# A decoder trunk on one core: VectorE's conditioning sums pinned in its order of issue, and spaced at 4500 columns in group B

## The chip, the cores and the metric

One core of a Trainium2 chip runs one program. The metric is the device time of one execution in microseconds, the median of a few runs of the same program. The engines are TensorE (PE: matmuls, with its weight loads listed as PEld), VectorE (DVE), ScalarE (ACT), GpSimd (POOL) and SyncE (SP), each with its own queue of instructions that it takes in order. SP issues most DMAs; POOL issues some.

## The reference, cut to what matters

One layer over 512 tokens of width 2048, batch 1, all in float32. The part that the change is about is the conditioning vector's product with a large matrix:

```python
c_act = jax.nn.silu(c)                    # (1, 2048)
mod = c_act @ w_mod[l] + b_mod[l]         # (1, 6 * 2048)
sh1, sc1, g1, sh2, sc2, g2 = split(mod, 6)
h = rms_norm(x, norm_attn[l]) * (1.0 + sc1) + sh1
...                                       # h @ w_in: queries and keys of groups A and B
x = x + g1 * (concat(out_A, out_B) @ w_out[l])
h = rms_norm(x, norm_ffn[l]) * (1.0 + sc2) + sh2
x = x + g2 * conv_ffn(h, w_up[l], conv_w[l], conv_b[l], w_down[l])
out = rms_norm(x, norm_final)
```

Group A is windowed attention of 16 heads; group B is attention of 16 heads over 128 keys for each query, chosen by an indexer (scores, then a top-k). The output projection is `w_out`, and the feed-forward part has 5632 hidden columns.

## The kernel before

Matrices are split into a high and a low part of a faster float type, and each product is three matmuls (`mm3`, L154). The weights come in tiles of 128x512 through a ring of buffers; ScalarE writes the high part, VectorE the low part (`split`, L147). TensorE takes the program's main stream of such tiles, "slots" (`drive`, L351), of 12 matmuls each: eight units of four slots for the queries of group A (qa0 to qa7), eight for group B (qb0 to qb7), sixteen for the output projection (wo0 to wo15), then the feed-forward part. Between slots generators advance by a step each. Attention runs as one of them: `pair_gen` (L802) takes two heads at a time through load, scores, softmax (VectorE adds the bias and takes the minimum into nm, ScalarE takes exp and divides), four-way transposes on TensorE (tpa, tpb), a copy by ScalarE to SBUF (eta, etb) and the product with the values (o). `prep_gen` (L881) makes keys kb and values vb of the next pair of B heads from wuk and wuv.

The conditioning product is cut into 24 groups of 512 columns (g = 0 to 23), each a sum of 16 pieces of 128x512. Groups 0 to 7 (shift and scale of the first norm) are done ahead of group A and don't concern us. For the others `mod_gen` (L233) loads a piece (tile mraw, 256 KB), and VectorE adds it, times one column of `cact`, to the accumulator macc (`mod_acc`, L199: L202 for the first piece, L204 for the other 15). After the sixteenth, `mod_cols` has TensorE add up macc's partitions in eight tiny matmuls (mps), and VectorE adds the bias (L251). Three such generators run:

- groups 8 to 13 beside group B of the attention (L1259): loads issued by POOL into the ring "mrw" of five buffers, so that piece n is loaded when the sum of piece n - 5 has given its buffer back. Groups 8 to 11 are the gate that the output projection needs.
- groups 14 to 19 beside the output projection (L1295): loads issued by POOL into eight buffers.
- groups 20 to 23 beside the feed-forward part (L1323): loads issued by SP into the ring "mrw" again.

`pace` (L266) sets at which point of the traced program a generator's step stands: each time that TensorE's counted columns have grown by a given number (5200, 3500 and 20000). But this is the place in the traced program alone. The framework's scheduler then puts each engine's instructions into their final order, by priority (the traced order) among those that its own estimate of times holds ready; an instruction whose operands it takes to be there early, as a sum whose block has been loaded, can be put far ahead of what was traced before it, and one that it takes for late can stand behind. The final order of each queue is fixed in the built program. On the chip each engine waits at the head of its queue for the semaphores of that instruction.

Of the kernel before, what the change touches and what calls it, by code (L numbers as in the profile page):

```python
# [11 lines left out]
OP = mybir.AluOpType  # L12
# [21 lines left out]
def hybrid_trunk(ctx, tc, xT, cT, wm, bm, nrm, wik, wiq, wi1, sinks, kvn, wuk, wuv, rel, onehot,  # L34
                 wo, wup, cw, cb, wdn, out):
    nc = tc.nc
    act, dve, pe, pool, sp = nc.scalar, nc.vector, nc.tensor, nc.gpsimd, nc.sync
# [63 lines left out]
    c_sb, sink_sb, bm_sb, nrm_sb = [t for t, _ in first.values()]  # L101
# [7 lines left out]
    cact = const.tile([P, KT], F32, name="cact")  # L109
# [5 lines left out]
    mod = const.tile([P, 24, 4], F32, name="mod")  # L115
# [83 lines left out]
    def mod_acc(accs, t, kt):  # L199
        acc = accs[kt % len(accs)]  # L200
        if kt < len(accs):
            dve.tensor_scalar(acc, t, cact[:, kt:kt + 1], None, OP.mult)  # L202
        else:
            dve.scalar_tensor_tensor(acc, t, cact[:, kt:kt + 1], acc, OP.mult, OP.add)  # L204

    def mod_rows(ps, t, q, start, stop):

# [9 lines left out]
    def mod_accs(g, mp, bufs, n=1):  # L217
        return [mp.tile([P, 512], F32, tag=f"macc{i}", bufs=1 if i else bufs, name=f"macc{g}_{i}") for i in range(n)]
# [14 lines left out]
    def mod_gen(groups, load, depth, mp, get, per):  # L233

        pieces = [(g, kt) for g in groups for kt in range(KT)]
        tiles = [load(*x) for x in pieces[:depth - 1]]
        n = 0
        for i, (g, kt) in enumerate(pieces):
            if i + depth - 1 < len(pieces):
                tiles.append(load(*pieces[i + depth - 1]))  # L240
            if kt == 0:
                acc = mod_accs(g, mp, 1)
            mod_acc(acc, tiles.pop(0), kt)
            n += 1
            if n % per == 0:
                yield
            if kt == KT - 1:
                ps = get(f"mps{g}")
                mod_cols(ps, acc)
                yield  # L250
                dve.tensor_tensor(mod[:, g], ps[:, 0:4], bm_sb[:, g], OP.add)  # L251


    active, idle = [], []
# [11 lines left out]
    def pace(gen, every):  # L266
        paced.append([gen, every, pe.cols])
# [29 lines left out]
    class Raw:  # L297
# [3 lines left out]
        def load(self, part):  # L301
            if part not in self.t:
                self.t[part] = load_raw(self.src[:, 512 * part:512 * part + 512], f"{self.name}_{part}")
# [264 lines left out]
    p1 = p1c.__enter__()  # L568
# [687 lines left out]
    drive(slots, marks["qb0"] - 4, marks["qb0"], True)  # L1256
    while idle:
        step()
    pace(mod_gen(range(8, 14), ring_mod, 5, p1, sc_ps, 1), 5200)  # L1259
    drive(slots, marks["qb0"], marks["wo"], True)  # L1260
    env["mh"] = mh = big.tile([P, KT, T], F32R, tag="b2", name="mh")
    env["ml"] = ml = big.tile([P, KT, T], F32R, tag="b3", name="ml")
# [158 lines left out]
```

## Time and profile before

| | us |
|---|---|
| median of 3 runs | 2219.88 (2218.86 to 2222.04) |
| profiled execution, its own time | 2221.85 |
| its span, first to last instruction | 2220.1 |

| stage (us of the span) | what TensorE works on |
|---|---|
| 0 to 186 | keys, indexer's queries, groups 0 to 7 of the conditioning |
| 186 to 386 | group A, indexer's scores and the top-k |
| 386 to 578 | group B |
| 578 to 800 | output projection, last heads of B at its start |
| 800 to 2220 | norm, feed-forward part, final norm |

The profile is read by stage: which engine is busy throughout, where that engine has idle time, and which instruction ended each idle time. The granted clock is TensorE's share of 2.4 GHz.

### The profile page before, as it was taken

To read this page: it belongs to the slowest core of one execution; us is meant where nothing else is said; L and a number is where in the kernel's file an instruction comes from. 1 tells how busy PE (TensorE), PEld (TensorE's weight loads), DVE (VectorE), ACT (ScalarE), POOL (GpSimd) and SP (SyncE) were. 2 spreads that over 40 slices of the span, in tenths; PEclk is the share of its full clock that TensorE was granted. 3 is DMA by queue.
4 is the path that set the end of the run, shared out by engine and by line. 5 is a ranking of instruction groups with operands and counts; after the bars stand their busy time and mean duration, and the time that the engine had idled before them with its cause. 6 is when DMAs were issued, how large, how long until landed. Compare 5 with 4: busy or idle time off the path is not lost.

```text
span 2220.1 us, 30149 instructions
## 1 busy us (share of the span) xinstructions
PE 2149.7 (97%) x10376; PEld 1750.1 (79%) x10376; DVE 1568.2 (71%) x2829; ACT 976.2 (44%) x1850; POOL 242.4 (11%) x376
## 2 busy tenths in 40 slices
PE   8999998999879999999999999999999999999997
PEld 4777776777768878888888888888888888888887
DVE  3887999566769765686867776675757666675666
ACT  5334877666722264334333343334334343333342
POOL 0000000111233200000201010110201010010200
PEclk9999999999989999999999999999999999999999
DMA  9783422454599734454757565563727465563672
GB/s 396 258 296 102 110 72 61 145 176 150 189 351 340 261 97 142 137 191 144 161 168 168 154 154 139 129 147 114 162 96 165 119 139 141 131 149 111 116 257 76
DMA packets 168921, 367.09 MB, mean 165 GB/s; under 512 B 20159, under 2 KB 27343, under 8 KB 162624
## 3 DMA queue, kind: packets, MB, share of 16 engines
q1 hardware_dynamic: 130208, 270.81, 36.9%
q0 software_dynamic: 37696, 92.79, 20.0%
q8 instruction: 81, 1.33, 0.2%
q10 hardware_dynamic: 864, 1.57, 0.2%
q14 instruction: 72, 0.59, 0.1%
HBM read 312.93 MB, written 52.17 MB: 164 GB/s over the span
## 4 chain that ended last, share of the span: by engine, by line
PE 79%; issue 13%; DMA 4%; DVE 2%; POOL 1%; ACT 1%; SPq 0%; POOLq 0%; DVEq 0%; ACTq 0%
PE p L53 17%; PE qip L53 3%; DMA mraw<-in_wm_dram 3%; POOL mraw L144 1%; PE ckv L53 1%; PE mps L53 1%; PE mrow L53 1%; DMA wiq<-in_wiq_dram 1%; DVE macc L204 1%; PE d_2ps L53 1%; PE u0ps L53 1%; PE g0ps L53 1%; PE d_0ps L53 1%; PE d_1ps L53 1%; PE wo15ps L53 0%
## 5 line engine op out<-in xcount | busy, mean ns | idle before, releaser
L190 ACT CAST dh<-rq 128x512 fp32r<-128x512 f32 x240 | 149.4, 623 | 172.0 <-PE p L53 140.5
L204 DVE SCALAR_TENSOR_TENSOR macc<-mraw,cact,macc 128x512 f32<-128x512 f32 x240 | 178.2, 748 | 39.4 <-DMA mraw<-in_wm_dram 36.5
L191 DVE TENSOR_TENSOR dl<-rq,dh 128x512 fp32r<-128x512 f32 x240 | 161.3, 685 | 40.0 <-ACT dh L190 39.1
L53 PE MATMUL p<-dh,ah 128*128 128x512 f32 x480 | 186.7, 389 | 0.0
L53 PE MATMUL p<-dl,ah 128*128 128x512 f32 x480 | 186.7, 389 | 0.0
L53 PE MATMUL p<-dh,al 128*128 128x512 f32 x480 | 186.7, 389 | 0.0
L1118 POOL DMA_DIRECT2D cd<-co x72 | 61.4, 858 | 878.6 <-DVE co L1131 876.2
L53 PEld LDWEIGHTS p<-dh,al 128*128 128x128 f32 x480 | 90.2, 188 | 18.7
L53 PEld LDWEIGHTS p<-dh,ah 128*128 128x128 f32 x480 | 90.1, 188 | 18.7
L53 PEld LDWEIGHTS p<-dl,ah 128*128 128x128 f32 x480 | 90.0, 188 | 18.8
L144 POOL DMA_DIRECT2D mraw<-in_wm_dram x96 | 51.6, 538 | 430.7 <-DVE macc L202 199.2
L1134 DVE TENSOR_TENSOR v<-p,v 128x512 f32<-128x512 f32 x120 | 82.3, 686 | 6.3 <-PE p L53 5.5
L1118 POOL DMA_DIRECT2D cd<-v x72 | 61.3, 856 | 128.4 <-DVE v L1136 76.2
L190 ACT CAST ah<-cu 128x256 fp32r<-128x256 f32 (+2 forms) x60 | 41.5, 692 | 50.5 <-DVE cu L1033 27.3
L1292 POOL DMA_DIRECT2D mraw<-in_wm_dram x96 | 51.4, 536 | 104.4 <-DVE macc L204 59.8
L191 DVE TENSOR_TENSOR al<-cu,ah 128x256 fp32r<-128x256 f32 (+2 forms) x60 | 46.7, 779 | 22.8 <-ACT ah L190 20.1
L1131 DVE TENSOR_TENSOR co<-p,v 128x512 f32<-128x512 f32 x80 | 54.9, 686 | 7.2 <-PE p L53 7.2
L1053 DVE TENSOR_TENSOR rq<-rq,rq 128x512 f32<-128x512 f32 x80 | 52.4, 685 | 1.4 <-DMA rq<-in_wdn_dram 1.4
L516 DVE TENSOR_TENSOR qi<-qi,qip 128x512 f32<-128x512 f32 x56 | 38.3, 684 | 14.4 <-PE qip L53 13.6
L778 ACT ACTIVATE sb<-sb,nmb 128x512 f32<-128x512 f32 (+2 forms) x64 | 35.3, 554 | 24.9 <-DVE nmb L776 21.4
L191 DVE TENSOR_TENSOR dl_t<-tw,dh_t 128x512 fp32r<-128x512 f32 x40 | 27.7, 692 | 22.5 <-ACT dh_t L190 22.5
L415 DVE SCALAR_TENSOR_TENSOR macc<-mraw,cact,macc 128x512 f32<-128x512 f32 x54 | 40.3, 747 | 0.4
(4492 smaller groups left out, 6396.2 us busy)
## 6 DMA issues: line engine op xcount, KB each, us to landing
mraw<-in_wm_dram POOLq DMA_DIRECT2D x192, 256.0 KB, 5.4
rq<-in_wdn_dram SPq DMA_DIRECT2D x160, 256.0 KB
mraw<-in_wm_dram SPq DMA_DIRECT2D x32, 1024.0 KB
cd<-co POOLq DMA_DIRECT2D x80, 256.0 KB, 4.8
cd<-v POOLq DMA_DIRECT2D x80, 256.0 KB, 4.7
mraw<-in_wm_dram SPq DMA_DIRECT2D x64, 256.0 KB
wiq<-in_wiq_dram SPq DMA_DIRECT2D x32, 256.0 KB
wik<-in_wik_dram SPq DMA_DIRECT2D x8, 592.0 KB
```

What stands on the lines that cost most here:

```text
L53: return self.to.matmul(out, w, x, **kw)
L144: by.dma_start(t, src)
L190: act.copy(hi_t, full)
L191: dve.tensor_tensor(lo_t, full, hi_t.bitcast(F32), OP.subtract)
L204: dve.scalar_tensor_tensor(acc, t, cact[:, kt:kt + 1], acc, OP.mult, OP.add)
L415: dve.scalar_tensor_tensor(acc, fetched[j, q][:, kt % 4], cact[:, kt:kt + 1], acc, OP.mult, OP.add)
L516: dve.tensor_tensor(qi[i], qi[i], ps, OP.add)
L1053: dve.tensor_tensor(self.b[out], self.b[a], self.b[b], OP.add)
L1118: pool.dma_start(cd[tb][dq], t, accum_op=OP.add)
L1131: dve.tensor_tensor(t, ps, box["v" if i == 1 else "u", b], OP.subtract)
L1134: dve.tensor_tensor(box["v", b], ps, box["v", b], OP.add)
L1292: pool.dma_start(t, wm[g, kt // 4][:, kt % 4])
```

## The change

`mod_acc`'s two forms of sum and the bias add of L251 are wrapped in `tc.keep_in_program_order`, which adds an edge without a semaphore: the scheduler must keep the instruction behind the one that was traced last before it on the same engine. This holds for groups 8 to 23. Instructions traced later can still be put ahead of a pinned one; nothing else is tied. And the generator beside group B takes its steps at every 4500 columns, where it was 5200. No operation is added or taken away.

```diff
--- before.py
+++ after.py
@@ -199,9 +199,9 @@
     def mod_acc(accs, t, kt):
         acc = accs[kt % len(accs)]
         if kt < len(accs):
-            dve.tensor_scalar(acc, t, cact[:, kt:kt + 1], None, OP.mult)
+            tc.keep_in_program_order(dve.tensor_scalar(acc, t, cact[:, kt:kt + 1], None, OP.mult))
         else:
-            dve.scalar_tensor_tensor(acc, t, cact[:, kt:kt + 1], acc, OP.mult, OP.add)
+            tc.keep_in_program_order(dve.scalar_tensor_tensor(acc, t, cact[:, kt:kt + 1], acc, OP.mult, OP.add))
 
     def mod_rows(ps, t, q, start, stop):
 
@@ -248,7 +248,7 @@
                 ps = get(f"mps{g}")
                 mod_cols(ps, acc)
                 yield
-                dve.tensor_tensor(mod[:, g], ps[:, 0:4], bm_sb[:, g], OP.add)
+                tc.keep_in_program_order(dve.tensor_tensor(mod[:, g], ps[:, 0:4], bm_sb[:, g], OP.add))
 
 
     active, idle = [], []
@@ -1256,7 +1256,7 @@
     drive(slots, marks["qb0"] - 4, marks["qb0"], True)
     while idle:
         step()
-    pace(mod_gen(range(8, 14), ring_mod, 5, p1, sc_ps, 1), 5200)
+    pace(mod_gen(range(8, 14), ring_mod, 5, p1, sc_ps, 1), 4500)
     drive(slots, marks["qb0"], marks["wo"], True)
     env["mh"] = mh = big.tile([P, KT, T], F32R, tag="b2", name="mh")
     env["ml"] = ml = big.tile([P, KT, T], F32R, tag="b3", name="ml")
```

Three places show how the built order moves. A name's last number is that of a buffer; `mraw9_12` is piece 12 of group 9.

VectorE in group B, near the end of group 9's sums. Names: macc is the accumulator, kb2 and qb2 are the keys and queries of the third pair's heads, `_l` are low parts of weights. Before:

```order
L204 SCALAR_TENSOR_TENSOR macc9_0_4147<-mraw9_10_4298,cact_99,macc9_0_4147 128x512
L204 SCALAR_TENSOR_TENSOR macc9_0_4147<-mraw9_11_4329,cact_99,macc9_0_4147 128x512
L204 SCALAR_TENSOR_TENSOR macc9_0_4147<-mraw9_12_4344,cact_99,macc9_0_4147 128x512
L602 TENSOR_TENSOR kb2_4268<-kbp2_4261,kb2_4268 64x512
L603 TENSOR_TENSOR kb2_4268<-kbp2_4261,kb2_4268 64x512
L587 SCALAR_TENSOR_TENSOR qb2_4280<-qb2ps_4029,qb2_4280 64x512
```

and with the change:

```order
L587 SCALAR_TENSOR_TENSOR qb2_4292<-qb2ps_4035,qb2_4292 64x512
L151 TENSOR_TENSOR qb3r_3l_4300<-qb3r_3_4158,qb3r_3h_4299 128x512
L602 TENSOR_TENSOR kb2_4277<-kbp2_4270,kb2_4277 64x512
L603 TENSOR_TENSOR kb2_4277<-kbp2_4270,kb2_4277 64x512
L204 SCALAR_TENSOR_TENSOR macc9_0_4089<-mraw9_8_4188,cact_99,macc9_0_4089 128x512
L587 SCALAR_TENSOR_TENSOR qb2_4292<-qb2ps_4035,qb2_4292 64x512
L204 SCALAR_TENSOR_TENSOR macc9_0_4089<-mraw9_9_4191,cact_99,macc9_0_4089 128x512
L151 TENSOR_TENSOR wuv2l_4331<-wuvr2_4147,wuv2h_4330 128x512
L204 SCALAR_TENSOR_TENSOR macc9_0_4089<-mraw9_10_4241,cact_99,macc9_0_4089 128x512
L151 TENSOR_TENSOR qb4r_0l_4347<-qb4r_0_4244,qb4r_0h_4346 128x512
L204 SCALAR_TENSOR_TENSOR macc9_0_4089<-mraw9_11_4256,cact_99,macc9_0_4089 128x512
L204 SCALAR_TENSOR_TENSOR macc9_0_4089<-mraw9_12_4286,cact_99,macc9_0_4089 128x512
```

Before, three sums stood in a row ahead of the first step of kb2; piece 12 stood seven rows behind piece 7, whose buffer its load takes. Now another instruction stands between any two of these sums, and piece 12 stands behind the steps of kb2 and qb2, 14 rows behind piece 7 (row 699, just ahead of these). Of the 80 pieces of groups 9 to 13, 19 stood at most nine rows behind the piece whose buffer they take; with the change 1 does (seven rows), and all others stand 14 rows or more behind. Group 8, whose sums stood in group A (rows 203 to 334 of VectorE's queue), has moved to the start of group B (617 to 670).

VectorE in the output projection, at the end of group 14. Before:

```order
L151 TENSOR_TENSOR wo4r_1l_6340<-wo4r_1_6291,wo4r_1h_6339 128x512
L204 SCALAR_TENSOR_TENSOR macc14_0_6145<-mraw14_14_6235,cact_99,macc14_0_6145 128x512
L204 SCALAR_TENSOR_TENSOR macc20_0_7961<-mraw20_5_8017,cact_99,macc20_0_7961 128x512
L204 SCALAR_TENSOR_TENSOR macc14_0_6145<-mraw14_15_6250,cact_99,macc14_0_6145 128x512
L151 TENSOR_TENSOR wo4r_2l_6366<-wo4r_2_6316,wo4r_2h_6365 128x512
L251 TENSOR_TENSOR mod_105<-mps14_6358,bm_sb_83 128x4
```

and with the change:

```order
L151 TENSOR_TENSOR wo4r_0l_6319<-wo4r_0_6262,wo4r_0h_6318 128x512
L204 SCALAR_TENSOR_TENSOR macc14_0_6145<-mraw14_14_6235,cact_99,macc14_0_6145 128x512
L151 TENSOR_TENSOR wo4r_1l_6340<-wo4r_1_6291,wo4r_1h_6339 128x512
L204 SCALAR_TENSOR_TENSOR macc14_0_6145<-mraw14_15_6250,cact_99,macc14_0_6145 128x512
L151 TENSOR_TENSOR wo4r_2l_6366<-wo4r_2_6316,wo4r_2h_6365 128x512
L251 TENSOR_TENSOR mod_105<-mps14_6358,bm_sb_83 128x4
```

Piece 5 of group 20 stood ahead of the last piece of group 14, and all sixteen pieces of group 20 stood in rows 969 to 1048, among those of groups 14 to 16. Now group 20 stands in rows 1220 to 1349, behind groups 14 to 19.

SP's queue, at the same place. Before:

```order
L144 DMA wo5r_2_6418<-in_wo_dram 128x512
L144 DMA mraw20_5_8017<-in_wm_dram 128x512
L144 DMA wo5r_3_6442<-in_wo_dram 128x512
L144 DMA mraw20_6_8081<-in_wm_dram 128x512
L144 DMA mraw20_7_8139<-in_wm_dram 128x512
L144 DMA wo6r_0_6466<-in_wo_dram 128x512
L144 DMA mraw20_8_8202<-in_wm_dram 128x512
```

and with the change:

```order
L144 DMA wo5r_2_6418<-in_wo_dram 128x512
L144 DMA wo5r_3_6442<-in_wo_dram 128x512
L144 DMA wo6r_0_6466<-in_wo_dram 128x512
L144 DMA wo6r_1_6494<-in_wo_dram 128x512
L1319 DMA x2d0_1659<-x2_0_6112 128x2048
L144 DMA wo6r_2_6519<-in_wo_dram 128x512
```

The loads of pieces 5 to 15 of group 20 and of pieces 0 to 4 of group 21 (16 loads of 256 KB) stood between the loads of wo5 to wo9. They now stand among those of the feed-forward part; pieces 0 to 4 of group 20 are still loaded at the start of the projection.

## Rows read from the trace of the kernel before

**Rows 1.** The page's first part: busy time of the span, its share and the number of instructions.

```profile
PE 2149.7 (97%) x10376; PEld 1750.1 (79%) x10376; DVE 1568.2 (71%) x2829; ACT 976.2 (44%) x1850; POOL 242.4 (11%) x376
```

**Rows 2.** The view of busy times in stretches that follow the stages (end of group A, group B, start of the output projection, its rest). Columns: stretch and its length, then busy us and instructions of each engine, the granted TensorE clock, the share of the DMA engines, GB/s.

```profile
186.00:386.00 200.00, 189.93 (x1079) 151.43 (x1077) 183.04 (x486) 150.79 (x387) 11.26 (x21) 0.98 0.32 88
386.00:578.00 192.00, 172.87 (x1046) 139.52 (x1045) 122.96 (x277) 127.74 (x304) 34.35 (x64) 0.95 0.55 168
578.00:660.00 82.00, 69.10 (x355) 54.66 (x356) 58.44 (x105) 35.44 (x76) 19.80 (x37) 0.88 0.76 275
660.00:800.00 140.00, 139.72 (x653) 116.53 (x652) 109.84 (x176) 40.01 (x64) 37.54 (x70) 1.00 0.79 272
```

**Rows 3.** The view of waits, TensorE alone, of 386 to 600 us: who waited for whom, us in total, times, the longest.

```profile
PE tpb L57 <- ACT etb L799: 8.7, 6, 2.6
PE o L53 <- ACT etb L799: 4.3, 2, 2.5
PE wo0ps L53 <- ACT mh L190: 3.3, 1, 3.3
PE kbp L53 <- DVE wuk7l L151: 3.0, 1, 3.0
```

**Rows 4.** The same view of TensorE, 600 to 800 us.

```profile
PE mps L53 <- DVE macc L204: 12.2, 2, 10.8
```

**Rows 5.** Busy times in the stretches in which the clock row of the profile shows 0.50, which is 1.2 of 2.4 GHz, with the same columns as rows 2.

```profile
444.80:448.20 3.40, 3.40 (x20) 2.97 (x15) 3.27 (x6) 1.17 (x2) 0.54 (x1) 0.50 0.29 100
496.00:499.40 3.40, 3.40 (x20) 2.35 (x20) 1.45 (x3) 0.87 (x2) 0.00 (x0) 0.50 0.29 104
530.10:533.50 3.40, 3.40 (x14) 3.11 (x13) 3.13 (x5) 1.17 (x2) 1.00 (x2) 0.51 0.46 158
574.50:584.70 10.20, 6.83 (x23) 5.36 (x21) 8.00 (x13) 8.66 (x18) 0.83 (x2) 0.50 0.42 137
646.20:659.80 13.60, 5.58 (x17) 4.83 (x18) 3.91 (x7) 0.08 (x1) 1.89 (x4) 0.50 0.88 314
```

**Rows 6.** The view of waits, VectorE alone, 386 to 600 us.

```profile
DVE macc L204 <- DMA mraw<-in_wm_dram: 21.5, 14, 3.6
...
DVE mod L251 <- PE mps L53: 2.3, 2, 1.6
```

**Rows 7.** The timeline of all engines, 439.5 to 444.5 us, in order of time: start, length, engine, line, operation, and in brackets the idle time before it and what ended that.

```profile
439.75 0.75 DVE L204 SCALAR_TENSOR_TENSOR macc<-mraw,cact,macc 128x512 f32<-128x512 f32 x1 [2.48 <-DMA mraw<-in_wm_dram]
...
440.42 0.68 DVE L602 TENSOR_TENSOR kb<-kbp,kb 64x512 fp32r<-64x512 f32 x1
...
441.82 0.58 ACT L599 CAST kb<-kbp 64x512 fp32r<-64x512 f32 x1 [2.44 <-DVE kb L603]
...
443.52 0.58 ACT L799 COPY etb<-tpb 128x512 f32<-128x512 f32 x1
...
444.15 0.55 PE L53 MATMUL o<-etb,vb 128*64 128x128 f32 x6 [1.87 <-ACT etb L799]
```

**Rows 8.** The timeline of all engines, 421 to 430 us: the first sum of group 9, the load that its buffer is next used for, and the sum that waits for that load.

```profile
421.74 0.48 DVE L202 TENSOR_SCALAR macc<-mraw,cact 128x512 f32<-128x512 f32 x1
...
422.52 0.56 POOL L144 DMA_DIRECT2D mraw<-in_wm_dram  x1 [127.39 <-DVE macc L202]
...
428.96 0.75 DVE L204 SCALAR_TENSOR_TENSOR macc<-mraw,cact,macc 128x512 f32<-128x512 f32 x1 [3.58 <-DMA mraw<-in_wm_dram]
```

**Rows 9.** The timeline of all engines, 637 to 657 us.

```profile
637.52 0.54 POOL L1292 DMA_DIRECT2D mraw<-in_wm_dram  x1 [0.18 <-issue]
...
640.82 0.43 SPq L144 DMA_DIRECT2D mraw<-in_wm_dram  x1
...
644.91 0.74 DVE L204 SCALAR_TENSOR_TENSOR macc<-mraw,cact,macc 128x512 f32<-128x512 f32 x1
...
652.66 1.42 DVE L204 SCALAR_TENSOR_TENSOR macc<-mraw,cact,macc 128x512 f32<-128x512 f32 x2 [7.01 <-DMA mraw<-in_wm_dram]
...
654.23 1.84 PE L53 MATMUL mps<-ones,macc 128*128 128x1 f32 x8 [10.77 <-DVE macc L204]
```

**Rows 10.** Busy times of 423 to 446 and 446 to 465 us, first of all instructions, then of those alone that read or write the accumulators macc (columns without POOL).

```profile
423.00:446.00 23.00, 18.57 (x115) 14.60 (x115) 16.17 (x33) 14.19 (x32) 6.51 (x13) 0.97 0.67 211
446.00:465.00 19.00, 19.00 (x122) 16.42 (x121) 8.94 (x27) 14.01 (x36) 1.61 (x3) 0.94 0.44 127
...
423.00:446.00 23.00, 0.00 (x0) 0.00 (x0) 8.26 (x12) 0.00 (x0) 0.97 0.67 211
446.00:465.00 19.00, 0.95 (x8) 1.05 (x8) 2.74 (x4) 0.00 (x0) 0.94 0.44 127
```

**Rows 11.** The DMA view of 600 to 660 us: GB/s in 40 slices of 1.5 us, and the last line of the view of tile mraw in 613 to 660 us and in 420 to 600 us (the time to landing of the loads that POOL issues).

```profile
GB/s 361 249 171 206 228 212 296 244 262 340 314 183 302 367 397 341 408 451 441 415 401 432 431 412 416 408 407 412 410 415 411 414 407 407 411 303 79 143 384 259
...
DMA to landing us min/median/max: 3.9/7.0/9.0
...
DMA to landing us min/median/max: 3.3/5.9/8.7
```

**Rows 12.** The view of tile mraw over the whole span: the sum on VectorE and the issue of the loads on POOL (shortest, median, longest in ns; first and last start).

```profile
L204 DVE SCALAR_TENSOR_TENSOR macc<-mraw,cact,macc x240: 722/749/755, 191.9 to 1283.0; 128x512 f32<-128x512 f32 x120
...
L144 POOL DMA_DIRECT2D mraw<-in_wm_dram x96: 536/536/613, 157.0 to 612.4; - x96
```

**Rows 13.** The view of waits, TensorE alone, of 186 to 386 us.

```profile
PE tpa L57 <- ACT sa L791: 5.3, 3, 2.9
```


## The prediction

> **What bounds the kernel now.** I read four views in this order: the page's busy times, the stretches by stage, the waits of TensorE by stage, and then the timeline at the longest waits. The first says that TensorE is busy 97% of the span [rows 1], so no edit of VectorE's queue can bring more than TensorE's idle time and its half-speed time. The stretches say where that is: TensorE was idle for 10 us of the 200 of group A, 19 us of the 192 of group B, 13 us of the 82 at the projection's start, and for next to nothing after 660 us [rows 2]. What TensorE waits for in each of these:
>
> - Group B and the start of the projection: transposes and products that need a copy by ScalarE (tpb 8.7, o 4.3), the first projection slot's wait for mh (3.3), keys that need the low part of wuk7 (3.0), 19.3 us together [rows 3].
> - Projection: the column sums mps wait for an accumulator, 1.4 us once and 10.8 us once [rows 4].
> - Group A's end: the transposes tpa, 5.3 us [rows 13], where VectorE is busy for 183 of 200 us [rows 2].
>
> Behind several of these the granted clock fell to 0.50, that is 1.2 GHz. Over those stretches TensorE was busy 3.40 (three times), 6.83 and 5.58 us [rows 5]; half of it is lost, 11.3 us in all: 5.1 in group B, 3.4 around the first projection slots, 2.8 behind the long mps wait.
>
> Who makes ScalarE late in group B? VectorE, mostly: its sums waited 21.5 us, in 14 waits, for their blocks [rows 6]. One instance is whole in the timeline: a sum waits 2.48 us for its DMA at 439.75, the step of kb behind it in VectorE's queue ends late, ScalarE's cast of kb has waited 2.44 us for it, the copy etb comes behind that in ScalarE's queue, and TensorE starts o 1.87 us late [rows 7]. The sum waits because five buffers are used faster than they come back: a buffer was free at 422.22, POOL issued its load at 422.52, and the sum that needed it began at 428.96, after 3.58 us of wait [rows 8]. Release to use is thus 6.7 us there. The sums come in clumps: 12 of them in 423 to 446 us, where TensorE is busy 18.6 of 23 us, and 4 in 446 to 465 us, where it is busy throughout [rows 10].
>
> **The change, part by part.**
>
> *1. Group B's waits.* With sums pinned at 4500 columns, one comes every 4500 / 2400 per us = 1.88 us of TensorE at full clock, and five buffers give a load 9.4 us from release to use. The row shows 6.7 us needed [rows 8], and POOL's loads here land in 3.3 to 8.7 us, median 5.9 [rows 11]. So most sums should find their block; the built order agrees, with one piece in 80 now close behind the one whose buffer it takes, against 19. At 5200 columns the loop would be 10.8 us, so the closer spacing costs some of the room, but not what is needed. Of tpb, o and kbp (16.0 us [rows 3]) I keep a quarter, since ScalarE also has waits of its own making, and the copies etb queue behind casts whatever VectorE does: −12. The bounds are 0 (ScalarE's own order is the cause) and −16. The mh wait is 3.3 us of group B's tail; half is taken: −1.6, bounds 0 and −3.3. The clock's loss goes with the waits ahead of it: three quarters of 5.1 + 3.4, −6.4, bounds 0 and −8.5.
>
> *2. Group 8 moves from A to B.* 16 sums of 0.73 us [rows 12], 11.7 us of VectorE. In B VectorE is idle 192 − 123 = 69 us [rows 2], so there they are covered; without that cover they would be on the path of etb like those above. In A they leave an engine that is 183 of 200 us busy, but they stood at that stage's start (the first at 191.9 [rows 12]), and TensorE waits at its end (5.3 us [rows 13]), so I take nothing: bounds −5.3 and 0.
>
> *3. The new waits in B.* A pinned bias add L251 waits for TensorE's mps, as it does now (2.3 us in two waits [rows 6]); behind it in VectorE's queue stand the next low parts and kb. And PE's mps comes close behind its sixteenth sum. In B no mps waited before; six of them now may. The nearest row is the shorter wait of the projection, 1.4 us [rows 4]; I take that for one or two of the six: +2, bounds 0 and 6 × 1.4 = +8.4.
>
> *4. The projection.* A sum of group 20 stood ahead of the last one of group 14. Its load was issued by SP at 640.82, into DMA queues that run at some 410 GB/s from 625 to 652 us [rows 9, 11]. VectorE waited 7.01 us for it; only then came the sum of group 14, and TensorE, whose wait of 10.77 us ended at 654.23, with mps14 [rows 9]. With group 20 out of the way, that sum waits for its own load, issued by POOL at 637.52 [rows 9]. POOL's loads landed here within 9.0 us at most [rows 11], by 646.5; with the sum and its successor mps begins by 648, where TensorE had arrived at 654.23 − 10.77 = 643.5. The remaining wait is 0 to 4 us; with the median landing of 7.0 it is nearly 2, which I take. So 12.2 us become 2 (−10.2, bounds −12.2 and −7), and the 2.8 us of half clock go, −2.8 (bounds −2.8 and 0).
>
> *5. SP's queue.* 16 loads of 256 KB leave the projection, 4.2 MB or 10 us at 410 GB/s, which is time that the weights' loads gain. But TensorE's long wait also let the loads run ahead: at 654 to 657 us the DMA engines fall to 79 and 143 GB/s, since the buffers were full [rows 11]. Without that rest a later slot or mps15 can come late. The nearest row is again the 1.4 us of mps [rows 4]; bounds 0 and +4, some three of these, and I take +2. The loads and sums of groups 20 and 21 go to the feed-forward part, where TensorE waits for nothing and VectorE has idle time throughout; the sums are spread over some hundred rows there. Cost nil; without that cover, 16 × 0.75 = 12 us.
>
> **Sum.** −12 − 1.6 − 6.4 + 2 − 10.2 − 2.8 + 2 = −29.0. The profiled execution took 2221.85 us, 2.0 above the median of 2219.88 and 1.75 above its own span of 2220.1. So 2192.9 by its own time, and 2190.9 against the median; I say 2191. With the better ends of parts 1, 3 and 4 (−16 − 3.3 − 8.5 − 12.2 − 2.8, no additions) it is −42.8; with B's waits and clock only halved (−8 − 1.6 − 4.2) and part 3 at 6.4 it is −18.4, or 2202. This case spans 2177 to 2203.
>
> **A rule of the Trainium skill against it.** POOL's issue of the loads lasted 536 ns in the shortest and the median case and 613 ns at the longest [rows 12], although VectorE is 64 to 78% busy in those stages [rows 2]. The Trainium skill, page "SBUF — State Buffer", section "SBUF: two separate sides", says that VectorE in a fast mode holds the port that GpSimd needs to write a DMA's descriptors, so that such a DMA stalls. By that rule, sums spread evenly over B would slow the very loads that feed them, and the time would be that of rival A2 below; by the row no issue was held up, and the trace so far speaks against it.
>
> **The rivals.**
>
> *A. B's waits stay, the projection's goes.* ScalarE's own order makes etb late: its copies stand behind casts that have other inputs too, and 4.3 us of o and 8.7 of tpb would stay. For it: one timeline is shown, not all eight waits. Against it: the waits sit where sums stand in clumps [rows 10]. It gives −10.2 − 2.8 + 2 and perhaps −4 of B, −15: 2205. Chance 0.17.
>
> *A2. Loads issued by POOL land later when sums are spread over all of B.* At the longest landing, 9.0 us [rows 11], with sum, issue and semaphores the loop takes some 10.4 us, 1 us over the 9.4 of the pace, so 0.2 us for each of 96 sums, 19 us of waits for VectorE, about the 21.5 of now [rows 6]. B gains little, and the time is A's, 2205. For it: 16 more loads come into B. Against it: the issue stays at 536 ns [rows 12], and the median landing was 5.9 us. Chance 0.05.
>
> *B. Slower: mps waits in each group of B.* In the pinned order TensorE's mps can stand in its queue ahead of the moment when VectorE reaches the sixteenth sum, since VectorE must first do what was traced before. TensorE then waits with all that is queued behind. The price of one lies between 1.4 and 10.8 us, mean 6.1 [rows 4], plus 1.7 of half clock (half of 3.40) [rows 5], 7.8 us; six would be 47, against the 29 + 2 gained elsewhere: 2220 − 31 + 47 = 2236. It decides from four of the six groups on. For it: what is pinned can no longer be moved ahead of a late step. Against it: VectorE is idle for 69 us in B. Chance 0.09.
>
> *C. Also A's end.* VectorE, freed of 11.7 us in A, comes to tpa earlier: another −5 to −10 with its clock, so 2170 to 2180 with the better ends. Chance 0.07.
>
> *D. No net change.* New waits as large as the old: 2220. Chance 0.07. That the change doesn't do what it says is excluded by the built order.
>
> **How the numbers follow.** Forecast 0.55 (2191, within 2177 to 2203), A and A2 together 0.22 (2205), B 0.09 (2236), C 0.07 (2174), D 0.07 (2220). The range of 8 in 10 takes in the forecast, nearly all of A and A2 and the upper part of C: 2175 to 2212. A measurement of this kernel can tell about 0.2%, 4.4 us, from no change. Faster: forecast, A, A2 and C make 0.84; 0.02 of A could end above 2215.5, so 0.82. Same: those 0.02 and most of D, 0.08. Slower: B and 0.01 of D, 0.10.
>
> **What would show it.** Part 1 is right if VectorE's waits of macc for DMA in group B fall from 21.5 to under 7 us and those of tpb, o and kbp to under 6; it is wrong if the first fall and the second stay (ScalarE's own order), or if the first stay (landing). Part 4 is right if no wait of mps is above 4 us and the clock stays at 1.0 around 650 us. Part 5 is wrong if a slot's weight or mps15 waits over 4 us after 660 us, or if TensorE has waits in the feed-forward part. B shows as six waits of mps in group B. What would make the whole wrong is a stall in a place that now has none.

## The result and the profile after

The kernel with the change took 2196.66 us (median of 5, 2192.5 to 2200.7), the kernel before 2220.55 us beside it (median of 5); the ratio is 0.9894, with a 95% interval of 0.9879 to 0.991. That is 23.9 us faster, where 29 were forecast; 2196.66 lies within the range. The profiled execution took 2198.84 us with a span of 2197.1, against 2221.85 and 2220.1 before: 23.0 us less, which is what the ledger below has to explain. One execution of one run below (2274.03 us, with groups 20 to 23 pinned, at a granted clock of 0.90) is left out of that run's figures.

The page's busy times are unchanged, as they must be, since no work was added [rows 1]:

```profile
PE 2147.9 (98%) x10376; PEld 1748.6 (80%) x10376; DVE 1566.8 (71%) x2829; ACT 975.7 (44%) x1850; POOL 242.2 (11%) x376
```

By stage (columns as in [rows 2]; the stages now end at 561, 634 and 778 us):

```profile
186.00:386.00 200.00, 192.14 (x1088) 153.46 (x1087) 176.37 (x477) 152.46 (x391) 3.45 (x7) 0.98 0.24 69
386.00:561.00 175.00, 168.46 (x1047) 135.98 (x1045) 132.33 (x291) 125.98 (x300) 43.98 (x82) 0.99 0.68 210
561.00:634.00 73.00, 68.00 (x347) 53.03 (x348) 50.95 (x93) 34.93 (x75) 17.66 (x33) 0.93 0.77 277
634.00:778.00 144.00, 142.54 (x676) 119.20 (x675) 106.34 (x170) 41.14 (x66) 37.55 (x70) 1.00 0.75 247
```

Group A lost 6.7 us of VectorE's time (183.04 to 176.37), group B and the projection's start got shorter, the rest of the projection is as before. TensorE's waits of 386 to 600 us, against [rows 3]:

```profile
PE tpb L57 <- ACT etb L799: 4.3, 6, 1.8
PE wo0ps L53 <- ACT mh L190: 2.7, 1, 2.7
PE o L53 <- ACT etb L799: 0.2, 1, 0.2
```

tpb has halved, o is nearly gone, kbp is gone; mh is little better. VectorE in the same stretch, against [rows 6]:

```profile
DVE macc L204 <- DMA mraw<-in_wm_dram: 6.0, 7, 2.2
DVE mod L251 <- PE mps L53: 3.7, 2, 2.5
```

21.5 us of waits for blocks have become 6.0. TensorE's waits of 600 to 800 us, against [rows 4]:

```profile
PE mps L53 <- DVE macc L204: 4.2, 1, 4.2
```

One wait of 4.2 us has taken the place of 1.4 and 10.8. The stretches at half clock, against [rows 5]:

```profile
366.90:370.20 3.30, 3.30 (x17) 3.30 (x17) 3.21 (x10) 2.17 (x5) 0.00 (x0) 0.50 0.00 0
380.60:387.30 6.70, 4.87 (x15) 3.61 (x16) 6.70 (x16) 3.42 (x12) 1.64 (x3) 0.50 0.53 142
513.70:517.00 3.30, 3.30 (x21) 2.55 (x20) 3.09 (x5) 0.48 (x1) 1.56 (x3) 0.50 0.49 132
561.50:564.80 3.30, 3.20 (x7) 2.21 (x8) 3.08 (x6) 3.24 (x7) 0.00 (x0) 0.50 0.38 123
626.30:633.00 6.70, 5.46 (x17) 4.71 (x18) 3.03 (x6) 0.00 (x0) 2.14 (x4) 0.50 0.96 344
2135.00:2138.30 3.30, 3.30 (x18) 3.30 (x17) 0.69 (x2) 0.00 (x0) 0.00 (x0) 0.50 0.02 5
```

In place of the three dips in B and the two long ones behind it there is one in B, one at wo0 and one behind mps, with 3.30, 3.20 and 5.46 us of busy TensorE. The second row is the dip at A's end, which was there before at 383 us; that at 366.9 is new, as one in A at 212.7 us is gone. The dip at 2135 lies in the feed-forward part, right behind a wait of 2.1 us for cu, a product of the convolution.

**The ledger**, from one profiled execution of each, by the starts of the first matmuls of qb0, wo0, wo4 and u0, and the end of the last matmul (the timeline):

| stage | before us | after us | difference |
|---|---|---|---|
| to qb0 (start and group A) | 357.91 | 354.40 | −3.5 |
| qb0 to wo0 (group B) | 220.68 | 207.08 | −13.6 |
| wo0 to wo4 (projection's start) | 81.29 | 72.39 | −8.9 |
| wo4 to u0 | 144.01 | 143.99 | 0.0 |
| u0 to the end | 1405.53 | 1408.56 | +3.0 |

The last row is scatter from one execution to the next: the same stage took between 1404.1 and 1408.7 us in the profiles of the twelve runs that follow, and no order of the sums goes with it; the wait for cu alone, 1.1 us before and 2.1 after, with the dip behind it, lies between 0.7 and 2.0 us in those.

### The profile page after: what moved, and what is told of

Same layout as the page of the kernel before. It is cut to its first block, busy times and chain, and to the rows that moved or that the text cites. A ratio compares the mean times of both kernels' runs of the same rounds, so it can differ in the third digit from the quotient of the medians.

```text
span 2197.1 us, 30169 instructions
## 1 busy us (share of the span) xinstructions
PE 2147.9 (98%) x10376; PEld 1748.6 (80%) x10376; DVE 1566.8 (71%) x2829; ACT 975.7 (44%) x1850; POOL 242.2 (11%) x376
## 4 chain that ended last, share of the span: by engine, by line
PE 85%; DVE 4%; ACT 3%; issue 3%; DMA 3%; POOL 1%; SPq 0%; DVEq 0%; POOLq 0%; ACTq 0%
PE p L53 17%; PE qip L53 4%; PE o L53 1%; PE ckv L53 1%; PE mrow L53 1%; PE mps L53 1%; POOL mraw L144 1%; DMA mraw<-in_wm_dram 1%; PE wo3ps L53 1%; DMA wiq<-in_wiq_dram 1%; PE scb L53 1%; PE u0ps L53 1%; DVE wk L661 1%; PE tpb L57 1%; PE d_2ps L53 1%
## 5 line engine op out<-in xcount | busy, mean ns | idle before, releaser
L516 DVE TENSOR_TENSOR qi<-qi,qip 128x512 f32<-128x512 f32 x56 | 38.3, 684 | 14.4 <-PE qip L53 13.6
```

The lines of the kernel that those rows point to most:

```text
L516: dve.tensor_tensor(qi[i], qi[i], ps, OP.add)
```

## The experiments

Each was timed beside the kernel before, and the ratio is to that. B is the time from qb0's first matmul to wo0's, and "waits" the time that VectorE waited for blocks of the sums within it, both of one profile.

| run | us | ratio, 95% interval | B us | waits us |
|---|---|---|---|---|
| before | 2219.88 | | 220.7 | 21.5 |
| the change | 2196.66 | 0.9879 to 0.9910 | 207.1 | 6.0 |
| pinned, 5200 | 2197.08 | 0.9883 to 0.9913 | 201.4 | 1.2 |
| 4500, not pinned | 2220.64 | 0.9994 to 1.0012 | 220.5 | 24.6 |
| 20 to 23 pinned, 5200 | 2212.78 | 0.9960 to 0.9984 | 218.7 | 19.2 |
| 8 to 13 pinned, 4500 | 2197.07 | 0.9892 to 0.9919 | 206.3 | 7.6 |
| late loads, pinned, 5200 | 2202.95 | 0.9920 to 0.9946 | 210.0 | 7.0 |
| threes, pinned | 2210.71 | 0.9947 to 0.9971 | 201.8 | 2.3 |
| loads of 20 to 23 pinned too | 2197.17 | 0.9886 to 0.9911 | 204.5 | 4.7 |
| mixed, 5200 | 2193.24 | 0.9872 to 0.9897 | 202.0 | 0.7 |
| pinned, 3600 | 2203.05 | 0.9911 to 0.9938 | 215.0 | 15.0 |
| 9 to 23 pinned, 4500 | 2200.52 | 0.9898 to 0.9924 | 206.4 | 5.5 |
| before, x2 late | 2211.47 | 0.9947 to 0.9977 | 220.5 | 19.8 |
| mixed, x2 late | 2195.92 | 0.9869 to 0.9904 | 202.2 | 1.7 |

### The parts apart

The pin alone (`4500` back to `5200`):

> The sums and bias adds pinned, the spacing left at 5200 columns. In the built order 11 of the 80 pieces of groups 9 to 13 stand at most nine rows behind the piece whose buffer they take (19 in the kernel before, 1 with both parts of the change). My theory (waits of VectorE for a block are what makes ScalarE's copies late; they come where a sum stands close behind the release of its buffer; the projection's stall comes of a sum of group 20 alone): VectorE's waits of macc for DMA in group B are about half of before, 10 us, tpb, o and kbp about 8, the mps wait 4, the time 2201 to 2207. Rival 1, the pin alone does it and the spacing nothing: 2194 to 2199. Rival 2, group B's gain comes of the spacing alone: tpb, o and kbp stay near 16, 2208 to 2212.

TensorE's waits of 386 to 600 us, then VectorE's for blocks:

```profile
PE tpb L57 <- ACT etb L799: 2.4, 5, 0.6
PE scb L53 <- DVE qb L587: 0.4, 1, 0.4
```

```profile
DVE macc L204 <- DMA mraw<-in_wm_dram: 1.6, 4, 0.9
```

2197.08 us: rival 1 had it, the pin alone brings the whole. My expectation counted how many sums stand close behind the release of their buffer in the built order (11 at 5200, 1 at 4500), and got the sign wrong: at 5200 VectorE waits less, not more, since a block has 10.8 us and not 9.4. B is even 5.7 us shorter than with 4500, but groups 12 and 13 end later, and the projection pays: its waits of mps are two, 6.9 us together, wo0 to wo4 takes 75.95 us against 72.39, and wo4 to u0 145.98 against 143.99.

The spacing alone (the three `keep_in_program_order` taken out, 4500 left):

> The spacing of 4500 columns without any pin. In the built order 12 of 80 pieces stand close behind the release of their buffer, group 8 stays in group A, and group 20's sums stand among those of groups 13 and 14. My theory: B's waits fall by about a third, the projection's stall stays (mps 8 to 12 us), the time 2208 to 2218. Rival 2 (spacing alone makes B's gain): 2203 to 2207. The rival that the early sums of group 20 do no harm: the mps wait is near 4 us and the time below 2203.

```profile
PE tpb L57 <- ACT etb L802: 7.2, 6, 2.1
PE o L53 <- ACT etb L802: 4.6, 3, 1.8
```

```profile
DVE macc L205 <- DMA mraw<-in_wm_dram: 24.6, 17, 3.4
```

2220.64 us, nothing. Without the pin the spacing does change the built order (12 of 80 pieces stand close, where 19 did), but VectorE's waits for blocks don't fall: 24.6 us, where they were 21.5. My expectation of a small gain was wrong; the stall of mps stayed in its place, at 6.8 us.

Groups 20 to 23 alone (`keep` for `g > 19`), and groups 8 to 13 alone (`keep` for `g < 14`, 4500):

> Only the sums and adds of groups 20 to 23 are pinned, spacing 5200: group B stands as before, group 20 moves behind the second norm. My theory: B's waits stay (tpb, o, kbp about 16 us), the mps wait falls from 10.8 to about 4 us, the gain is 7 to 10 us, 2210 to 2214. Rival (the stall of mps comes of the saturated DMA, and group 20's sum only happened to stand there): mps stays at 9 to 11 us, under 3 us of gain, 2217 to 2221.

> Only groups 8 to 13 are pinned, spacing 4500: group B stands as with the whole change, group 20 stays early, among groups 13 to 15. My theory: B's waits as with the whole change (tpb, o, kbp about 4.5 us, macc for DMA about 6), the mps wait of the projection stays at 8 to 12 us, 2203 to 2208. Rival (group 20 does no harm): 2195 to 2200. Together with the run that pins group 20 alone the gains should add up to the whole, 23.9 us within 4.

With group 20 out of the projection (TensorE, 600 to 800 us):

```profile
PE mps L53 <- DVE macc L205: 4.2, 2, 2.2
```

The stall of 10.8 us is gone and B is as before; the gain of 7.5 us is as expected. But with groups 8 to 13 pinned alone the whole gain is there, 2197.07, though group 20 still stands among groups 13 to 15. The timeline of that run:

```profile
631.29 1.70 PE L53 MATMUL mps<-ones,macc 128*128 128x1 f32 x8 [2.65 <-DVE macc L205]
...
636.84 1.63 DVE L205 SCALAR_TENSOR_TENSOR macc<-mraw,cact,macc 128x512 f32<-128x512 f32 x2 [5.70 <-DMA mraw<-in_wm_dram]
```

Its mps14 waits 2.65 us. The first twelve pieces of group 20 stand ahead of piece 10 of group 14 there, and the long wait for a block (5.70 us) comes only after mps14, where TensorE waited for nothing. So the two gains don't add up (7.5 + 23.2 is 31, not 24), against my expectation: each takes away the same stall of the projection.

### What in group B: waits or clumps

What holds up TensorE, a wait for a block or several sums in a row by themselves? One run is meant to have the waits without more clumps, one the clumps with few waits. The first (an excerpt of its edit):

```diff
+        turns = list(range(len(pieces)))
+        if groups[0] == 8:
+            for k in range(6, 90, 12):
+                turns[k:k + 4] = [k + 1, k + 2, k + 3, k]
...
-                tiles.append(load(*pieces[i + depth - 1]))
+                j = turns[i + depth - 1]
+                tiles[j] = load(*pieces[j])
```

> All pinned and spaced at 5200 columns, so that VectorE's order is that of the run that pinned at 5200 (2197.1 us, 1.6 us of waits for blocks and 2.8 us of TensorE's waits for etb and keys in group B); but in groups 8 to 13 every twelfth block is loaded after the three that follow it (the loads, too, pinned in POOL's order), so that it has two sums' spacing, 4.3 us, instead of five from the release of its buffer to its use. This puts waits for a DMA of some 2.5 us each under 8 sums without clumping any. Theory (waits for blocks make B's stalls): VectorE waits 15 to 25 us for blocks in group B, TensorE's waits for etb and keys rise by 6 us or more, the time is 2205 to 2214. Rival (the clumps of sums, each 2 us and more of VectorE's own work in a row, make them): VectorE waits as much, TensorE's waits stay under 5 us, 2195 to 2200.

```profile
PE tpb L57 <- ACT etb L806: 4.0, 5, 1.8
...
PE mps L53 <- DVE macc L206: 1.5, 1, 1.5
PE kbp L53 <- DVE wuk2l L153: 1.1, 1, 1.1
```

```profile
DVE macc L206 <- DMA mraw<-in_wm_dram: 7.3, 6, 3.0
```

The late loads made 7.0 us of waits in B, not 15, and the time lies between the two figures: 2202.95 us, slower than the run at 5200 with intervals that don't touch. B took 8.6 us more (210.0 against 201.4) for 5.8 us more of waits; VectorE's order differs from that run's by seven moved rows, and both have 73 sums in B. TensorE's waits for etb, keys and queries rose from 2.8 to 5.5 us (0.4 of each is scb), mps added 1.5, and half clock in B rose from 6.8 to 17.1 us. So waits for blocks make stalls in B, at this order of the queue.

The second run:

```diff
-    pace(mod_gen(range(8, 14), ring_mod, 5, p1, sc_ps, 1), 4500)
+    pace(mod_gen(range(8, 14), ring_mod, 5, p1, sc_ps, 3), 15600)
```

> All pinned, but group B's sums traced in threes at every 15600 columns (three times 5200): clumps of about three sums, 2.2 us of VectorE's work at one place, with five buffers as ever, of which a block has 8 us and more from release to use. Theory (waits for blocks make B's stalls): few waits for blocks (under 6 us), TensorE's waits in group B stay under 6 us, 2195 to 2201. Rival (the clumps themselves): waits for blocks are few, but TensorE's waits for etb and keys rise by 6 us or more, 2205 to 2212.

```profile
PE tpb L57 <- ACT etb L799: 3.3, 5, 1.3
```

```profile
DVE macc L204 <- DMA mraw<-in_wm_dram: 2.3, 3, 1.2
```

B took 201.8 us, as at 5200 (201.4), with 3.3 us of waits of tpb. But as a test of clumps this run is weak: the sums are traced in threes, yet in VectorE's queue other instructions stand between most of them. In B 22 of 66 sums start less than 1 us behind the one before, against 24 of 73 at 5200 and 28 of 64 in the kernel before.

The run's 2210.71 us, which I had not expected, come behind B. Ten sums of group 13 stand in a row in the projection, from 599.5 to 611.2 us (two rows of VectorE's timeline, then TensorE's waits of 600 to 800 us):

```profile
604.57 0.75 DVE L204 SCALAR_TENSOR_TENSOR macc<-mraw,cact,macc 128x512 f32<-128x512 f32 x1 [2.78 <-DMA mraw<-in_wm_dram]
605.58 3.11 DVE L204 SCALAR_TENSOR_TENSOR macc<-mraw,cact,macc 128x512 f32<-128x512 f32 x4 [0.26 <-DMA mraw<-in_wm_dram]
...
PE mps L53 <- DVE macc L204: 16.4, 2, 12.8
```

They are 7.5 us of VectorE's work and 4.0 us of waits for blocks, and mps13, which adds up what they make, waits 12.8 us. So where TensorE waits for the sum itself, a row of sums does cost.

The spacing closer still (`4500` to `3600`):

> The whole change with a spacing of 3600 columns in place of 4500: a sum every 1.5 us, five buffers give a block 7.5 us from release to use (9.4 at 4500, 10.8 at 5200). VectorE's waits for blocks in group B were 1.6 us at 5200 and 6.0 at 4500. Theory (the room of the five buffers decides): they rise to 15 us or more, TensorE's waits for etb and keys to 8 or more, 2202 to 2212. Rival (spacing is free as long as the sums are pinned, as between 5200 and 4500): 2194 to 2199.

```profile
PE tpb L57 <- ACT etb L799: 8.7, 5, 2.2
...
PE kbp L53 <- DVE wuk3l L151: 1.7, 1, 1.7
```

```profile
DVE macc L204 <- DMA mraw<-in_wm_dram: 15.0, 15, 3.1
```

2203.05 us, as the theory had it. At 5200, 4500 and 3600 columns, which leave a block 10.8, 9.4 and 7.5 us, VectorE waits 1.2, 6.0 and 15.0 us and B takes 201.4, 207.1 and 215.0 us. Over all fourteen profiles of the table a straight line gives B = 201 us + 0.9 us for each us of VectorE's waits for blocks (correlation 0.98).

Two rivals can be held against this line. A closer spacing also brings more sums into B (73, 84 and 96 in these three); but with group 8 left out of B (the next section) there are 68 in place of 84, and B takes 206.4 us against 207.1. And the clumps: a line through the ten runs that pin groups 9 to 13 alone (200.6 us + 0.98 for each us) gives 219 to 225 us for the four runs that don't, where 218.7 to 220.7 were measured. So the waits account for the whole of what B loses in those four, and nothing is left that clumps would have to explain, though no run here has long rows of sums in B with all their blocks present.

### Group 8 and group A

> The whole change, but group 8 not pinned: its sums go back into group A (rows 203 to 334 of VectorE's queue), all else stands as with the change. Theory: TensorE's short waits in A for dots and sca come back, 2 us, and A takes 1.7 to 3.5 us more, the rest as with the change: 2198 to 2201. Rival (group 8 out of A is worth nothing, as I predicted, and its 16 sums more in B cost something there): 2192 to 2197.

The short waits of TensorE in 186 to 386 us in the kernel before, and with group 8 put back into A:

```profile
PE dots L53 <- DVE wic L619: 1.2, 1, 1.2
PE sca L53 <- ACT relu L633: 0.5, 1, 0.5
PE dots L53 <- ACT relu L633: 0.3, 1, 0.3
PE dots L53 <- DVE nma L776: 0.2, 1, 0.2
```

```profile
PE dots L53 <- DVE wic L622: 1.2, 1, 1.2
PE sca L53 <- ACT relu L636: 0.6, 1, 0.6
...
```

and with the change, in the same stretch:

```profile
PE tpa L57 <- ACT sa L791: 4.5, 3, 2.3
...
PE tpa L57 <- ACT eta L799: 0.7, 2, 0.4
```

With group 8 out of A the waits of dots and sca, 2.2 us, are gone, and they come back with it; tpa at A's end stays (4.5 and 0.7 against 5.3). The time went to 2200.52 us, 3.9 more than with the change, as the theory had it, though the intervals overlap. The start and group A (to qb0) took 5.3 us more in this one profile, and not 1.7 to 3.5. The other profiles bear the gain out: the first matmul of qb0 starts at 356.7 to 359.7 us, 358.4 in the mean, in the five with group 8 in A, and at 354.4 to 356.9, 355.5 in the mean, in the nine without.

### What is left in the projection

The loads of groups 20 to 23 pinned in SP's order too (`tc.keep_in_program_order(load)`):

> The whole change, and the loads of groups 20 to 23 also pinned in SP's order, so that the first five of group 20 (1.3 MB, some 3 us of the DMA engines at 410 GB/s) leave the start of the projection for its end. Theory (what is left of the mps wait, 4.2 us, comes of group 14's own blocks landing late under a full DMA): the wait falls by 1 to 3 us, 2193 to 2197. Rival (VectorE's own work ahead of group 14's last sum): unchanged, 2195 to 2199.

VectorE's waits for blocks of 558 to 630 us in this run:

```profile
DVE macc L206 <- DMA mraw<-in_wm_dram: 6.0, 6, 2.1
```

2197.17 us, and mps waits 4.2 us, as without this edit. That is the rival's figure, but the run doesn't decide between the two: the edit did not bring group 14's blocks sooner, whose sums wait 6.0 us for them, as with the change (5.9 us in six waits, 603 to 616 us). The run at 5200 decides more: there no sum waits over 0.3 us for a block in 560 to 670 us, and mps14 still waits 4.3 us.

Then three loads of the residual, 1 MB each, issued later:

```diff
-        n = (1,1,4)[i - 1]
+        n = (8, 14, 16)[i - 1]
         drive(slots, at, at + n, True)
-        sp.dma_start(env["x2"][i], xT[i])
+        tc.keep_in_program_order(sp.dma_start(env["x2"][i], xT[i]))
```

> The kernel before, nothing pinned but three loads on SP: those of the residual's blocks 1 to 3 (1 MB each, needed when the output projection reaches its fifth, ninth and thirteenth unit) are issued after 14, 28 and 44 of its 64 tiles in place of 7, 8 and 12. This takes 3 MB, some 7.5 us of the DMA engines at 410 GB/s, out of the stretch ahead of the 10.8 us wait of mps, and leaves group 20's sum ahead of group 14's last. Theory (the stall needs both, the sum's place and a full DMA): VectorE's 7.0 us wait shrinks to 3 us or less, mps waits 5 us or less, 2211 to 2216. Rival (the place alone): mps stays over 8 us, 2217 to 2222.

The kernel before with this one edit: TensorE's waits of 600 to 800 us, and VectorE's for blocks of 600 to 660 us:

```profile
PE mps L53 <- DVE macc L205: 3.9, 2, 2.4
```

```profile
DVE macc L205 <- DMA mraw<-in_wm_dram: 6.5, 6, 1.8
```

Two pieces of group 20 still stand between the last ones of group 14, yet the longest wait for a block is 1.8 us where it was 7.0, mps waits 2.4 us at most where it was 10.8 [rows 4, 9], and the time is 2211.47 us, 8.4 less, as the theory had it. Its reason isn't shown, though. The DMA view of 600 to 660 us of this run (GB/s in 40 slices of 1.5 us), and the issue on SP of the load in question, piece 5 of group 20:

```profile
GB/s 223 212 214 239 201 288 239 227 328 396 193 325 374 367 281 380 442 407 397 302 251 311 352 392 402 396 302 332 408 415 417 408 417 397 399 397 427 412 339 350
...
623.59 0.38 SPq L144 DMA_DIRECT2D mraw<-in_wm_dram  x1
```

Two things changed with this edit. The DMA engines move 250 to 402 GB/s from 630 to 642 us, where it was 401 to 432, and some 400 from there to 657 us, as before [rows 11]. And the load has another place: in SP's queue it stands behind the second load of wo4, no longer behind the third of wo5, and SP came to it at 623.59 us, not at 640.82 [rows 9], 17 us sooner. So the stall was a sum placed ahead of group 14's last one whose block came late; how much of that is the late issue and how much the full DMA stays open. The run with groups 8 to 13 pinned fits: there, too, group 20 is early both in VectorE's queue and in SP's, and mps14 waits 2.65 us.

The mixed version (`keep` for `g < 14 or g > 19`, 5200, loads of 20 to 23 pinned), without and with the later loads of the residual:

> What seems best so far: groups 8 to 13 and 20 to 23 pinned, 14 to 19 not; spacing 5200; the loads of groups 20 to 23 pinned in SP's order. Group B as in the run that pinned all at 5200, the projection as in the run that pinned groups 20 to 23 alone (4.2 us of mps wait, half clock for 3.4 us in place of 6.8) or a little better. Theory: 2192 to 2196. Rival (groups 14 to 19 have to be pinned too, since unpinned sums wait for blocks ahead of the weights' low parts): 2197 to 2203.

> The mixed version (groups 8 to 13 and 20 to 23 pinned, spacing 5200, the loads of 20 to 23 pinned; 2193.2 us) with the residual's loads 1 to 3 moved as in the run on the kernel before. Theory (what is left of mps14's wait and of the half clock behind it comes of group 14's blocks under a full DMA): the waits of mps fall from 5.3 to under 2 us, 2188 to 2192. Rival (VectorE's own work ahead of that sum): 2192 to 2195.

2193.24 us, as the theory had it, and 2195.92, above both figures: both intervals overlap that of the change, so neither is shown to be better, and moving the residual's loads, worth 8 us in the kernel before, is worth nothing here. The timeline of the second, a cast of ScalarE, VectorE's two idle times and TensorE's mps14:

```profile
607.12 0.62 ACT L152 CAST wo3r_0h<-wo3r 128x512 fp32r<-128x512 f32 x1 [7.55 <-DMA wo4r<-in_wo_dram]
...
607.77 0.69 DVE L153 TENSOR_TENSOR wo3r_0l<-wo3r,wo3r_0h 128x512 fp32r<-128x512 f32 x1 [4.33 <-ACT wo3r_0h L152]
...
612.26 0.75 DVE L967 SCALAR_TENSOR_TENSOR x<-wo0ps,mod,x 128x512 f32<-128x512 f32 x1 [2.35 <-DMA x<-in_xT_dram]
...
628.28 1.02 PE L53 MATMUL mps<-ones,macc 128*128 128x1 f32 x8 [2.39 <-DVE macc L207]
```

The waits of mps there are 2.66 us (mps13) and 2.39 us (mps14), 5.3 us together in the run without the later loads, though in both runs no sum waits for a block in 600 to 670 us. VectorE stood 4.33 us until ScalarE had written wo3r_0h, whose cast had itself waited for a DMA, and 2.35 us until a block of x had landed; it had no other idle time over 0.3 us from 603 us until mps14. So the rest of the wait isn't the landing of the sums' blocks but what stands ahead of the last sum in VectorE's queue: work, and waits for weights and for x. How much of it is due to the full DMA stays open, and what would shorten it was not tried.

## Why the prediction was right, step by step

- **Part 1, B's waits: right, and its size.** tpb, o and kbp fell from 16.0 to 4.5 us, −11.5 where −12 was forecast. The cause is shown by the late loads (the waits alone added) and by the three spacings. What I named as evidence against rival A, that the sums come in clumps [rows 10], was a poor reason: with the change, too, 27 of 84 sums in B start less than 1 us behind the one before, and B's time goes with the waits alone. Rival A is refuted: TensorE's waits for etb went with VectorE's waits for blocks. The test that I had set, waits for blocks under 7 us and tpb, o and kbp under 6, was met. mh was mis-sized: −0.6, not −1.6.
- **The clock: mis-sized.** I let it go with the waits, −6.4 in B and around wo0 and −2.8 behind mps. There TensorE is still busy at half clock for 3.30 + 3.20 + 5.46 = 12.0 us where it was 22.6 [rows 5]; half of the difference is −5.3, not −9.2. The dip behind mps stayed nearly whole, 5.46 us where it was 5.58, though the wait fell from 10.8 to 4.2 us. And half is too much: TensorE's busy time up to u0's first matmul, for the same 3976 matmuls, fell by 3.5 us only (before, then after; columns as in [rows 2]):

```profile
0.00:803.90 803.90, 749.36 (x3976) 582.94 (x3977) 607.37 (x1272) 424.01 (x948) 111.02 (x216) 0.97 0.61 205
0.00:777.86 777.86, 745.90 (x3976) 579.81 (x3977) 597.10 (x1256) 423.52 (x948) 110.71 (x216) 0.98 0.61 206
```

- **Part 1's spacing: the direction right, the size not.** That 4500 costs some of the five buffers' room was said, but "not what is needed" failed: against 5200 VectorE waits 6.0 us for blocks, not 1.2, and B takes 5.7 us more, which the projection gives back. That the change would be as fast without it (2197.08 us) was not said. The pin is the change.
- **Part 2, group 8: failed.** "I take nothing" looked at tpa at A's end alone, and that did stay. The gain lay earlier in A: 2.2 us of dots and sca.
- **Part 3, new waits in B: none.** L251 went from 2.3 to 3.7 us on VectorE, and TensorE waits for no mps in B; rival B is refuted. +2 was not needed.
- **Part 4, the projection: right, a little short.** mps went from 12.2 to 4.2 us, −8.0 where −10.2 was taken; 4.2 is just over the bound of 4 that I gave. The test set for it, no wait of mps over 4 us and no dip around that place, was missed by little in the wait and outright in the dip (626.3). The reason given for the bound, that the last sum waits for its own block, failed: with the change VectorE has no idle time over 0.1 us from 616.7 us until that sum. It is late by earlier waits and by its other work. That POOL's loads land within 9.0 us failed too: the ten that it issues from 598 to 610 us take 9.2 to 16.1 us. With the blocks there in time 4.3 us of wait stay at 5200, and 2.39 in the mixed version.
- **Part 5, SP's queue: nothing came late** in the projection behind wo4, and +2 was not needed. TensorE does wait in the feed-forward part, against what the prediction reads: 1.1 us for cu before and 2.1 after, and for the final norm 3.0 us before and 3.3 after. The feed-forward part took the sums of group 20 at no cost that can be told from scatter.
- **Rival A2, loads issued by POOL:** the issue over the whole span and the landing of the loads of 386 to 561 us, against [rows 11, 12]:

```profile
L144 POOL DMA_DIRECT2D mraw<-in_wm_dram x96: 536/536/570, 157.1 to 578.3; - x96
...
DMA to landing us min/median/max: 3.1/5.4/8.2
```

The issue stayed at 536 ns in the median (570 at the longest), with VectorE busy for 132 of 175 us in B, where it was 123 of 192. In B the median landing is 5.4 us where it was 5.9, and the longest 8.2 where it was 8.7, so the rival's landing of 9.0 us did not come. By the Trainium skill's page "SBUF — State Buffer", section "SBUF: two separate sides", a fast mode of VectorE stalls DMAs that GpSimd issues; these sums, with two float32 operands in SBUF, don't show that. Whether they run in such a mode no run here shows.

Summed: the waits, −11.5 − 0.6 − 8.0 − 2.2, are −22.3, and TensorE's idle time up to u0 fell by 22.6 us (54.5 to 32.0, length less busy time in the two rows above), so they are nearly all of it. With −3.5 of busy time it is −26.0, and with the feed-forward part's +3.0 of this execution −23.0, as measured. Taken by halves, −5.3, the clock would leave 1.6 us too much.

That the sum of −29.0 came out this near is in part luck: the clock, taken at −9.2, gave −3.5, and against that stand the two additions of +2 that were not needed and group 8's −2.2 that was not foreseen.

## What to carry to other kernels

A filler step that reads from a small ring of buffers is harmless only while its own data are there: look first for its waits on the DMA in the engine's queue, then for its work, and compare the time from a buffer's release to its next use with the landing of a load. Work counts, too, where another engine waits for the step's own result, as mps13 did for ten sums in a row. A scheduler that fills by estimate can put such steps together or ahead of their data; pinning them at evenly traced places was worth 23 us of 2220 here, while a closer spacing without the pin was worth nothing. Where two edits each remove the same stall (here group 20's place, and the times around it), their gains don't add up. And a gain of one stage can be lost in the next: at 5200 columns group B is 5.7 us shorter than at 4500, and the kernel is no faster.

## What the runs showed of the hardware that was not expected

A wait of VectorE for a block lengthened group B by about as much as it lasted, 0.9 us for each us, though VectorE itself had idle time of 69 us in that stage [rows 2]. A part of the price is TensorE's clock: in B it was at 1.2 GHz for 21.1 us in the kernel before, 17.1 with the late loads, 13.7 with the change and 6.8 with all pinned at 5200. In the kernel with the change every stretch at half clock between 300 and 700 us comes right behind a wait of TensorE: 2.29 us ahead of the dip at 366.9, 1.75 and 2.27 around that of 380.6, 1.79 ahead of 513.7, 2.70 ahead of 561.5, 4.21 around 627.5; behind the waits of 0.37 to 0.80 us in that time the clock stayed at 2.4 GHz. The reverse doesn't hold in every run: at 5200 no such stretch follows a wait of 2.28 us that ends at 369.2. The stretch around the long wait of mps had 5.58 us of busy TensorE with a wait of 10.8 us and has 5.46 with one of 4.2, so shortening that wait gave almost nothing of the clock back.
